# At two joins, token tiles finished one after the other, transposed between the last two weights' products, with three engines in written order

## Chip, cores and metric

The kernel runs on one core of one Trainium2 chip. The metric is the device time of one execution in microseconds (us); the median of several runs is compared. Engine names in the profile: PE is TensorE's products, PEld its weight loads, DVE is VectorE, ACT is ScalarE, POOL is GpSimd, SP is the queue that issues most transfers.

## Reference

Two layers over 512 tokens of 1024 values, all in float32. Each sub-layer is `x <- LayerNorm(ALPHA * x + sublayer(x))`. Layer 0 is a gated DeltaNet mixer and a dense SwiGLU; layer 1 is an S5 state-space mixer and a top-2-of-8 mixture of SwiGLU experts.

```python
def layer_norm(x, g, b):
    mu = mean(x); var = mean((x - mu)**2)
    return (x - mu) * rsqrt(var + LN_EPS) * g + b

def swiglu(x, w1, w3, w2):
    return (silu(x @ w1) * (x @ w3)) @ w2

# layer 0
h = gdn_mixer(x, ...)                        # ends in: o @ w_out
x = layer_norm(ALPHA * x + h, g00, b00)      # first join
f = swiglu(x, w1, w3, w2)                    # ends in: hidden @ w2
x = layer_norm(ALPHA * x + f, g01, b01)      # second join
# layer 1
h = s5_mixer(x, ...)                         # begins with: x @ s5_w_in
...
```

## The kernel before

Tokens lie in four tiles of 128 rows (`L.r[t]`, 128 x 1024 each). Every float32 operand of a product is kept as two parts: a high part (`hi`, fp32r, written by ScalarE, L68 or L73 for weights) and a low part (`lo` = value - high, written by VectorE, L69 or L76). A product of two such operands is three TensorE products (`mm3`, L128 to L130): high x high, high x low, low x high.

Weights come in 1 MB blocks of 128 x 2048. SP loads one into a `wraw` buffer (L104, three buffers here), then `wsplit` writes `whi` and `wlo` from it (two places each, so a block's high part can only be written when the products with the block two before it are done). `wload` does all of it.

At both places that the text calls joins, a matrix product ends a sub-layer and another begins the next. At the first join the last two blocks of `w_out` (high and low parts of the attention output `oT`, in the buffers `aTh` and `aTl`) give the right half of each row, at L166 and L167; then `ffn_first` (L803) starts the feed-forward layer with its first two weight blocks, f = 0 and 1. At the second join the last two blocks of `w2` end the feed-forward layer (`ffn_last`, L854) and `s5` (L1059) starts with two blocks of `s5_w_in`.

The function `two` (L181) is the join:

- it multiplies tiles 0 and 1 with both weights, then calls `res` (residual add and statistics, L692 and L727) and `ln_rows` (L752: some ten steps on one column, L734 to L750, then the row itself, L754) for them;
- it multiplies tiles 2 and 3, and turns tiles 0 and 1 with `ln_cols` (L771): 16 transposes of 128 x 128 (L781) into four PSUM buffers, and per 128 columns a ScalarE step that applies gain and offset (L785, into one of four `tmp`), the high part (L68) and the low part (L69) into `aTh` and `aTl`. These two have one place each; at the first join it is the place of `oT`'s parts;
- it calls `res` and `ln_rows` for tiles 2 and 3, which `ln_cols` turns later, when the next products are half through (the second half of `ffn_first` and of `s5`). A half is 96 products of 256 columns.

The scheduler, a list scheduler that fills each engine's instruction stream by priority and its own cost model, sets the order on all engines. Into the same streams it puts two other things near the first join. One is `ln_own` (L788): the row tiles times gain plus offset, L790 and L791, which the next residual needs and nothing before it. The other is `s5_prep` (L878), woven with the feed-forward layer by `weave`: powers of complex numbers on VectorE (L916 to L926), a chain of 113 GpSimd steps from the cosine on (L957 to L968, and L981 to L983), then on VectorE products `u` (L1021, L1023) and `w1` (L1025). The large tile `w1` of L1010 has the name of the GpSimd chain's scratch `w1` (L955), and one place with it: its first write waits for the chain's last read of the scratch (L965).

Each engine works off its stream in order; an instruction waits for the semaphores of what it needs, and all behind it wait with it.

Of the kernel before, what the change touches and what calls it, by code (L numbers as in the profile page):

```python
# [10 lines left out]
F32 = mybir.dt.float32  # L11
FR = mybir.dt.float32r
# [3 lines left out]
AF = mybir.ActivationFunctionType  # L16
# [3 lines left out]
P = 128  # L20
# [6 lines left out]
PE, DVE, ACT = (getattr(mybir.EngineType, n) for n in ("PE", "DVE", "Activation"))  # L27
# [31 lines left out]
class Builder:  # L59
# [82 lines left out]
    def build(self):  # L142
        tc, i = self.tc, self.i
        sb = lambda name, **k: tc.tile_pool(name=name, bufs=1, reuse_waits="tile", **k)
        with ExitStack() as es:
            self.wp = es.enter_context(sb("wp"))
            self.wpools = [(self.wp, dict(raw=2, hi=2, lo=2), None)]
            self.wcount = dict(raw=0, hi=0, lo=0)
            self.early = []
            self.share, self.after = 0, None  # L150
            self.cp = es.enter_context(sb("const"))
            self.pp = es.enter_context(tc.tile_pool(name="psum", bufs=1, space=bass.MemoryType.PSUM))
            act = es.enter_context(ExitStack())
            self.ap_ = act.enter_context(sb("act", side="right"))
            with sb("gdn") as self.gp:
                oT, ps0 = self.gdn()
            w = [self.wload(i["w_out"][2 + q]) for q in range(2)]
            self.rp = es.enter_context(sb("row"))
            self.wmore(es, "wmid", 1, 0, 0)
            r = self.rows("xp")  # L160
            L = self.ln_begin(r, 0)
            with sb("ffn") as self.fp, sb("prep") as self.sp:
                ps1 = [self.psum("pa") for t in range(4)]
                for t in range(4):
                    self.residual(L, t, 0, ps0[t], ALPHA)
                res = lambda t: self.residual(L, t, 1, ps1[t], ALPHA)  # L166
                self.two(lambda ts: self.tok_mm(ps1, oT, w, ts), res, L)  # L167
                first = self.ffn_first(L)
                self.weave((self.ffn(L, first), 1.0), (self.s5_prep(), PREP))
                L = self.ffn_last()  # L170
            with sb("s5") as self.sp:
                glu = self.s5(L)
            with sb("moe") as self.mp, ExitStack() as ws:
                self.wmore(ws, "wx", *WX)
                self.glu(L, *glu)
                act.close()
                self.share = SHARE
                with sb("mx", side="right") as self.mx:
                    self.moe(self.L3)

    def two(self, mm, res, L):  # L181


        mm((0, 1))
        for t in (0, 1):
            res(t)
            self.ln_rows(L, t)
        mm((2, 3))
        self.ln_cols(L, 0)
        for t in (2, 3):  # L190
            res(t)
            self.ln_rows(L, t)

    def consts(self):
        nc, cp = self.nc, self.cp
# [573 lines left out]
            g.tensor_add(r, r, L.gr[:, 1])  # L769

    def ln_cols(self, L, half, tag="acc"):  # L771
        s, v, pe = self.nc.scalar, self.nc.vector, self.nc.tensor
        if half == 0:
            L.xT = tuple(self.ap_.tile([P, KB, T], FR, name=n, tag=n, bufs=1) for n in ("aTh", "aTl"))
        cs = slice(256 * half, 256 * half + 256)
        for b in range(4):
            ps = self.psum(tag, (P, 2, 256))
            for j in range(2):
                k = 2 * b + j
                for t in range(2):  # L780
                    pe.transpose(ps[:, j, t * P:(t + 1) * P], L.r[2 * half + t][:, k * P:(k + 1) * P], self.ident)  # L781
            for j in range(2):
                k = 2 * b + j
                tmp = self.rp.tile([P, 256], F32, name="tmp", bufs=4)
                s.activation(tmp, ps[:, j], AF.Identity, scale=L.gc[:, 0, k:k + 1], bias=L.gc[:, 1, k:k + 1])  # L785
                self.split(tmp, L.xT[0][:, k, cs], L.xT[1][:, k, cs])

    def ln_own(self, L, t):  # L788
        v = self.nc.vector
        v.tensor_mul(L.r[t], L.r[t], L.gr[:, 0])  # L790
        v.tensor_add(L.r[t], L.r[t], L.gr[:, 1])  # L791
# [8 lines left out]
                         k == 0, k == KB - 1)  # L800
                yield 650 * (cs.stop - cs.start) // 512

    def ffn_first(self, L):  # L803

        w = [self.wload(self.i["ffn13"][f]) for f in range(2)]
        ps = [[self.psum("pa") for _ in range(2)] for f in range(2)]
        for half in range(2):
            if half:
                self.ln_cols(L, 1)
            for f in range(2):  # L810
                for _ in self.ffn_up(w[f], L.xT, ps[f], slice(256 * half, 256 * half + 256)):
                    pass
        return ps
# [43 lines left out]
    def ffn_last(self):  # L857

        py = [self.psum("acc") for _ in range(4)]
        for _ in self.ffn_down(py, self.ffn_w2(1, 1, 0), 0, range(4)):  # L860
            pass
        w = [self.ffn_w2(1, 1, f0) for f0 in (4, 8)]

        def mm(tiles):
            for n in range(2):
                for _ in self.ffn_down(py, w[n], 4 + 4 * n, tiles):
                    pass
        self.two(mm, lambda t: self.residual(self.L2, t, 1, py[t], 1.0), self.L2)
        return self.L2

# [183 lines left out]
                                          ap=[[128, 8], [3584, 16], [1, 128]]), tp[:, e].rearrange("p c t -> p (c t)"))  # L1056
            yield 2000

    def s5(self, L):  # L1059


        S = SimpleNamespace(un=self.sp.tile([P, 16, 8, 16], F32, name="un"), c={}, U={}, X={}, y={})
        ps = [[self.psum("pa", (P, 2, 256)) for _ in range(2)] for _ in range(2)]
        w = [self.wload(self.i["s5_w_in"][Q]) for Q in range(2)]
        S.c[0] = self.s5_load(0)
        for half in range(2):
            if half:
# [390 lines left out]
    def moe(self, L):  # L1458
# [28 lines left out]
        with self.order(DVE, ACT):  # L1487
# [24 lines left out]
            rows(0)  # L1512

            ov, two, rem, rc, a, b, bq, t0 = (c8(x) for x in ("ov", "two", "rem", "rc", "a", "b", "bq", "t0"))
            v.tensor_scalar(two, q, float(PAIRS), None, op0=OP.is_lt)
            v.scalar_tensor_tensor(ov, two, -float(RM), n, op0=OP.mult, op1=OP.add)
            v.tensor_scalar(rem, ov, 128.0, None, op0=OP.is_gt)
            for m in (256.0, 384.0):
# [460 lines left out]
```

## Time and profile before

| | us |
|---|---|
| runs (median, lowest, highest of 3) | 1459.57, 1453.78, 1462.43 |
| the profiled execution, its own time | 1465.39 |
| its span, first to last instruction | 1463.4 |
| TensorE busy (PE) | 1411.5 (96%) |
| VectorE busy | 964.5 (66%) |
| ScalarE busy | 701.5 (48%) |
| GpSimd busy | 547.0 (37%) |
| mean granted TensorE clock | 0.976 |

Times of the profile count from the span's first instruction. The first join lies at about 345 to 396 us, the feed-forward layer reaches to about 740, the second join lies at about 740 to 792. A busy time is the union of an engine's instructions in the stretch. The granted clock is 1.00 at 2.4 GHz and 0.50 at 1.2 GHz. In a timeline, what stands in brackets is the time for which the engine was idle before the row, and the instruction that ended the idle time.

### The profile page before, as it was taken

The page shows a single profiled execution, that of the slowest core. Times are in us where ns is not written, and L with a number is a line of the kernel's source. Part 1 is how long each engine was busy: PE and PEld are TensorE (multiplying, and loading weights), DVE is VectorE, ACT ScalarE, POOL GpSimd, SP SyncE. Part 2 cuts the span into 40 slices and gives each one's busy share as a digit, 9 for nine tenths or more (in the row PEclk, how much of TensorE's full clock was granted, in tenths as well). Part 3 has the DMA queues.
Part 4 walks back from the last instruction along what each step waited for, and adds up shares of the span by engine and source line. Part 5 has one row for each costly group of instructions (what it writes and reads, how often), then busy time and mean ns, then how long its engine had stood idle before and what let it go on. Part 6 is the DMA issues. An engine that isn't in the chain of part 4 may idle for free. (4 is left out here: it accounts for less than half of the span.)

```text
span 1463.4 us, 26997 instructions
## 1 busy us (share of the span) xinstructions
PE 1411.5 (96%) x10724; PEld 1178.7 (81%) x10724; DVE 964.5 (66%) x1675; ACT 701.5 (48%) x938; POOL 547.0 (37%) x660
## 2 busy tenths in 40 slices
PE   8999999999999999999999999998999999999994
PEld 5878787777877777777878878788998899999883
DVE  5757587637976666653356486686864587778793
ACT  5636365433534434443234323255764577776540
POOL 1000000000787773000000830036975579988250
PEclk9989999879999999999999999999999999999997
DMA  5221222205334454443235766378975799997861
GB/s 205 62 66 62 66 64 66 68 30 182 116 117 152 155 165 153 144 134 123 90 132 222 220 218 240 123 297 329 393 277 202 265 393 398 363 383 280 279 224 38
DMA packets 97747, 274.15 MB, mean 187 GB/s; under 512 B 33472, under 2 KB 51024, under 8 KB 78032
## 3 DMA queue, kind: packets, MB, share of 16 engines
q1 hardware_dynamic: 92688, 256.29, 48.9%
q0 software_dynamic: 4928, 16.08, 3.8%
q8 instruction: 86, 1.41, 0.4%
q14 instruction: 45, 0.37, 0.1%
HBM read 241.47 MB, written 30.88 MB: 186 GB/s over the span
## 5 line engine op out<-in xcount | busy, mean ns | idle before, releaser
L76 DVE TENSOR_TENSOR wlo<-wraw,whi 128x2048 fp32r<-128x2048 f32 (+2 forms) x165 | 353.2, 2147 | 150.2 <-ACT whi L73 150.2
L73 ACT ACTIVATE whi<-wraw 128x2048 fp32r<-128x2048 f32 (+1 forms) x165 | 309.1, 1877 | 219.3 <-PE acc L130 88.6
L128 PE MATMUL pa<-whi,xgh 128*128 128x256 f32 x704 | 205.3, 292 | 0.3 <-ACT whi L73 0.3
L129 PE MATMUL pa<-wlo,xgh 128*128 128x256 f32 x704 | 197.9, 281 | 4.9 <-POOL wlo L78 4.9
L130 PE MATMUL pa<-whi,xgl 128*128 128x256 f32 x704 | 198.2, 282 | 0.9 <-DVE xgl L69 0.9
L78 POOL TENSOR_TENSOR wlo<-wraw,whi 128x384 fp32r<-128x384 f32 x73 | 172.4, 2381 | 44.5 <-ACT whi L73 41.6
L128 PE MATMUL pa<-aTh,whi 128*128 128x512 f32 (+1 forms) x400 | 154.4, 389 | 1.6 <-ACT aTh L68 1.5
L130 PE MATMUL pa<-aTh,wlo 128*128 128x512 f32 (+1 forms) x400 | 154.2, 387 | 1.3 <-DVE wlo L76 1.3
L129 PE MATMUL pa<-aTl,whi 128*128 128x512 f32 (+1 forms) x400 | 153.2, 385 | 1.5 <-DVE aTl L69 1.5
L128 PEld LDWEIGHTS pa<-whi,xgh 128*128 128x128 f32 x704 | 133.1, 189 | 11.2 <-issue 8.1
L128 PE MATMUL acc<-whi,hh 128*128 128x512 f32 x352 | 140.9, 401 | 0.0
L130 PE MATMUL acc<-whi,hl 128*128 128x512 f32 x352 | 139.0, 397 | 0.8 <-DVE hl L69 0.7
L129 PEld LDWEIGHTS pa<-wlo,xgh 128*128 128x128 f32 x704 | 133.5, 190 | 7.0 <-POOL wlo L78 5.2
L129 PE MATMUL acc<-wlo,hh 128*128 128x512 f32 x352 | 138.9, 395 | 0.0
L130 PEld LDWEIGHTS pa<-whi,xgl 128*128 128x128 f32 x704 | 133.1, 189 | 1.3 <-DVE xgl L69 1.3
L128 PE MATMUL acc<-aTh,whi 128*128 128x512 f32 x240 | 101.2, 422 | 7.3 <-ACT whi L68 6.9
L129 PE MATMUL acc<-aTl,whi 128*128 128x512 f32 x240 | 101.0, 421 | 0.0
L130 PE MATMUL acc<-aTh,wlo 128*128 128x512 f32 x240 | 100.1, 417 | 0.0
L129 PEld LDWEIGHTS pa<-aTl,whi 128*128 128x128 f32 x400 | 76.5, 192 | 17.5 <-DVE aTl L69 2.0
L128 PEld LDWEIGHTS pa<-aTh,whi 128*128 128x128 f32 x400 | 76.1, 191 | 17.8 <-ACT aTh L68 2.1
L130 PEld LDWEIGHTS pa<-aTh,wlo 128*128 128x128 f32 x400 | 76.4, 192 | 16.9 <-DVE wlo L76 2.2
L130 PEld LDWEIGHTS acc<-whi,hl 128*128 128x128 f32 x352 | 65.7, 188 | 18.0 <-DVE hl L69 2.9
(513 smaller groups left out, 2860.1 us busy)
## 6 DMA issues: line engine op xcount, KB each, us to landing
wraw<-in_m SPq DMA_DIRECT2D x95, 1024.0 KB
wraw<-in_ffn SPq DMA_DIRECT2D x30, 1024.0 KB
r<-in_m SPq DMA_DIRECT2D x22, 1024.0 KB
wraw<-in_w_in SPq DMA_DIRECT2D x15, 1024.0 KB
grow<-in_m SPq DMA_DIRECT2D x11, 1024.0 KB
c<-s_d SPq DMA_DIRECT2D x8, 1024.0 KB
wraw<-in_w_glu SPq DMA_DIRECT2D x8, 1024.0 KB
c<-s_d SPq DMA_DIRECT2D x8, 768.0 KB
```

The costliest lines, as they stand in the source:

```text
L73: self.nc.scalar.activation(hi, src, AF.Copy)
L76: self.lo = self.nc.vector.tensor_sub(lo[:, :m], src[:, :m], hi[:, :m].bitcast(F32))
L78: self.nc.gpsimd.tensor_sub(lo[:, m:], src[:, m:], hi[:, m:].bitcast(F32))
L128: mm(out, a[0], b[0], start=start, stop=False)
L129: mm(out, a[0], b[1], start=False, stop=False)
L130: return mm(out, a[1], b[0], start=False, stop=stop)
```

## The change

`two` now takes the products per weight (`mm(tiles, n)`), loads the next two weights itself, and writes three engines' instructions in a fixed relative order (`self.order(DVE, PE, ACT)`). Tile 0 is multiplied with both weights, then normed; then tile 1. Tiles 2 and 3 are multiplied with the first weight; the 16 transposes of tiles 0 and 1 come next, all of them before the columns; then the next weight's split and three of four column steps, the products with the second weight, the second next weight's high part, the fourth column step, both residuals, its low part, and the row norms. Instructions from outside the block (`ln_own`, `s5_prep`) are still put between these by the scheduler.

```diff
-    def two(self, mm, res, L):
-        mm((0, 1))
-        for t in (0, 1):
-            res(t)
-            self.ln_rows(L, t)
-        mm((2, 3))
-        self.ln_cols(L, 0)
-        for t in (2, 3):
-            res(t)
-            self.ln_rows(L, t)
+    def two(self, mm, res, L, nxt, tag):
+        v, s = self.nc.vector, self.nc.scalar
+        raws = [self.wraw(x) for x in nxt]
+        w = [(self.wtile("hi", FR), self.wtile("lo", FR)) for _ in nxt]
+        mms = lambda *a: [None for _ in mm(*a)]
+        hi = lambda n: s.activation(w[n][0], raws[n], AF.Copy)
+        lo = lambda n: v.tensor_sub(w[n][1], raws[n], w[n][0].bitcast(F32))
+        with self.order(DVE, PE, ACT):
+            for t in (0, 1):
+                mms((t,), 0)
+                mms((t,), 1)
+                res(t)
+                self.ln_rows(L, t)
+            mms((2, 3), 0)
+            hi(0)
+            lo(0)
+            cols = self.ln_turned(L, 0, tag)
+            for b in range(3):
+                next(cols)
+            mms((2, 3), 1)
+            hi(1)
+            next(cols)
+            for t in (2, 3):
+                res(t)
+            lo(1)
+            for t in (2, 3):
+                self.ln_rows(L, t)
+        return w
...
     def ln_cols(self, L, half, tag="acc"):
+        for _ in self.ln_turned(L, half, tag):
+            pass
+
+    def ln_turned(self, L, half, tag):
         s, v, pe = self.nc.scalar, self.nc.vector, self.nc.tensor
...
-        for b in range(4):
-            ps = self.psum(tag, (P, 2, 256))
+        pt = [self.psum(tag, (P, 2, 256)) for b in range(4)]
+        for b, ps in enumerate(pt):
             for j in range(2):
...
+        for b, ps in enumerate(pt):
             for j in range(2):
                 k = 2 * b + j
                 tmp = self.rp.tile([P, 256], F32, name="tmp", bufs=4)
                 s.activation(tmp, ps[:, j], AF.Identity, scale=L.gc[:, 0, k:k + 1], bias=L.gc[:, 1, k:k + 1])
                 self.split(tmp, L.xT[0][:, k, cs], L.xT[1][:, k, cs])
+            yield
```

`ffn_first` and `s5` get the two split weights from `two` instead of loading them. In SP's queue this moves the row constants of the second norm behind three blocks of the feed-forward layer, and the fourth block of `s5_w_in` ahead of six loads of S5 tables; all else there stays.

Three places show the move in the built program. Line numbers in rows of the changed kernel are its own (L190 is L76 of before, L816 and L817 are L790 and L791, L938 to L948 are L916 to L926, L956 is L934, L1043, L1045, L1047 are L1021, L1023, L1025).

**PE, first join.** `pa_3508` and `pa_3509` are the right halves of tiles 0 and 1; `whi_3474`, `wlo_3475` the first, `whi_3480`, `wlo_3481` the second weight. In the kernel before, PE's stream reads here:

```order
L128 MATMUL pa_3508<-whi_3474,aTh_3240 128x512
L129 MATMUL pa_3508<-wlo_3475,aTh_3240 128x512
L130 MATMUL pa_3508<-whi_3474,aTl_3241 128x512
L128 MATMUL pa_3509<-whi_3474,aTh_3240 128x512
L129 MATMUL pa_3509<-wlo_3475,aTh_3240 128x512
L130 MATMUL pa_3509<-whi_3474,aTl_3241 128x512
L128 MATMUL pa_3508<-whi_3480,aTh_3240 128x512
L129 MATMUL pa_3508<-wlo_3481,aTh_3240 128x512
L130 MATMUL pa_3508<-whi_3480,aTl_3241 128x512
```
In the changed kernel it reads:

```order
L129 MATMUL pa_3508<-wlo_3475,aTh_3240 128x512
L130 MATMUL pa_3508<-whi_3474,aTl_3241 128x512
L128 MATMUL pa_3508<-whi_3474,aTh_3240 128x512
L129 MATMUL pa_3508<-wlo_3475,aTh_3240 128x512
L130 MATMUL pa_3508<-whi_3474,aTl_3241 128x512
L128 MATMUL pa_3508<-whi_3480,aTh_3240 128x512
L129 MATMUL pa_3508<-wlo_3481,aTh_3240 128x512
L130 MATMUL pa_3508<-whi_3480,aTl_3241 128x512
L128 MATMUL pa_3508<-whi_3480,aTh_3240 128x512
```
The second weight is met after tile 0's own products with the first, instead of after those of both tiles: 7 products behind the first that starts at 345.19 us in the profile of before, where it was 19.

**DVE, first join, behind the norm of tile 1.** `wlo_3525` (before: `wlo_3725`) is the low part of the next weight, the rows with `aTl` are the low splits of the turned columns, `pw`, `t1`, `t2` belong to the S5 preparation, the rows with `grow` are the own scaling. In the kernel before, VectorE's stream reads here:

```order
L908 TENSOR_TENSOR cn_4036<-cn_4036,rr_4016 128x32
L76 TENSOR_TENSOR wlo_3725<-wraw_3722,whi_3724 128x2048
L692 SCALAR_TENSOR_TENSOR r_3491<-r_3491,pa_3510 128x512
L692 SCALAR_TENSOR_TENSOR r_3491<-r_3491,pa_3511 128x512
L727 BN_STATS b6_3501<-r_3491 128x6 x2
L734 BN_AGGR lnst_3500<-b6_3501 128x2
L76 TENSOR_TENSOR wlo_3731<-wraw_3728,whi_3730 128x2048
L69 TENSOR_TENSOR aTl_3643<-tmp_3649,aTh_3642 128x256
L69 TENSOR_TENSOR aTl_3643<-tmp_3653,aTh_3642 128x256
L69 TENSOR_TENSOR aTl_3643<-tmp_3662,aTh_3642 128x256
L69 TENSOR_TENSOR aTl_3643<-tmp_3666,aTh_3642 128x256
```
In the changed kernel it reads around the first low part:

```order
L816 TENSOR_TENSOR r_3490<-r_3490,grow_3498 128x1024
L190 TENSOR_TENSOR wlo_3525<-wraw_3520,whi_3524 128x2048
L938 TENSOR_TENSOR pw_4045<-er_4017,cn_4039 128x32
L939 TENSOR_TENSOR pw_4045<-er_4017,sn_4038 128x32
L817 TENSOR_TENSOR r_3490<-r_3490,grow_3498 128x1024
L943 TENSOR_TENSOR t1_4050<-pw_4045 128x32
L944 TENSOR_TENSOR t2_4051<-pw_4045 128x32
L956 TENSOR_SCALAR rr_4019<-pw_4045 128x32
L816 TENSOR_TENSOR r_3490<-r_3490,grow_3498 128x1024
L69 TENSOR_TENSOR aTl_3631<-tmp_3652,aTh_3630 128x256
L945 TENSOR_TENSOR pw_4045<-t1_4050,t2_4051 128x32
L817 TENSOR_TENSOR r_3490<-r_3490,grow_3498 128x1024
```
Both next low parts stood ahead of the splits, four of which came in a row; the own scaling came after all eight. Now all four steps of the own scaling of tiles 0 and 1 stand ahead of the second split, and 33 small steps of the preparation stand between the first low part and the eighth split.

**DVE, first join, second half.** The splits of tiles 2 and 3 in the changed kernel, with `u1`, `u2` and `w1` of the preparation:

```order
L1043 TENSOR_TENSOR u1_4626<-pw_4045,bb_4625 128x4x128
L1045 TENSOR_TENSOR u2_4627<-pw_4045,bb_4625 128x4x128
L69 TENSOR_TENSOR aTl_3631<-tmp_3857,aTh_3630 128x256
L69 TENSOR_TENSOR aTl_3631<-tmp_3861,aTh_3630 128x256
L1047 TENSOR_TENSOR w1_4638<-u1_4626,u2_4627 128x4x128
L816 TENSOR_TENSOR r_3491<-r_3491,grow_3498 128x1024
L69 TENSOR_TENSOR aTl_3631<-tmp_3865,aTh_3630 128x256
L69 TENSOR_TENSOR aTl_3631<-tmp_3869,aTh_3630 128x256
L69 TENSOR_TENSOR aTl_3631<-tmp_3873,aTh_3630 128x256
L69 TENSOR_TENSOR aTl_3631<-tmp_3877,aTh_3630 128x256
```
In the kernel before, the same splits, from the third on:

```order
L69 TENSOR_TENSOR aTl_3643<-tmp_3852,aTh_3642 128x256
L69 TENSOR_TENSOR aTl_3643<-tmp_3856,aTh_3642 128x256
L926 TENSOR_TENSOR pw_4042<-t1_4047,t2_4048 128x32
L791 TENSOR_TENSOR r_3491<-r_3491,grow_3498 128x1024
L69 TENSOR_TENSOR aTl_3643<-tmp_3865,aTh_3642 128x256
L69 TENSOR_TENSOR aTl_3643<-tmp_3869,aTh_3642 128x256
L921 TENSOR_TENSOR t1_4047<-pw_4042 128x32
L69 TENSOR_TENSOR aTl_3643<-tmp_3878,aTh_3642 128x256
L69 TENSOR_TENSOR aTl_3643<-tmp_3882,aTh_3642 128x256
L922 TENSOR_TENSOR t2_4048<-pw_4042 128x32
```
The `w1` step stands between the second and the third split now. Before, it came after the eighth split and two further low parts.

## Rows read from the trace of the kernel before

**Rows 1.** The page, part 1: engine, busy us (share of the span), instructions.
```profile
PE 1411.5 (96%) x10724; PEld 1178.7 (81%) x10724; DVE 964.5 (66%) x1675; ACT 701.5 (48%) x938; POOL 547.0 (37%) x660
```

**Rows 2.** Busy time by stretch: length, then PE, PEld, DVE, ACT, POOL; clock, DMA.
```profile
366.51:382.76 16.25, 14.02 (x114) 13.43 (x113) 16.21 (x57) 8.12 (x18) 7.47 (x15) 1.00 0.36 129
382.76:396.40 13.64, 12.79 (x102) 12.10 (x101) 13.40 (x34) 11.11 (x21) 13.06 (x29) 1.00 0.10 30
420.00:440.00 20.00, 18.72 (x82) 14.49 (x80) 17.33 (x24) 8.18 (x8) 16.13 (x32) 1.00 0.59 182
440.00:740.00 300.00, 300.00 (x1421) 239.50 (x1420) 163.24 (x229) 110.77 (x153) 100.86 (x253) 1.00 0.43 138
760.18:776.50 16.32, 14.14 (x102) 13.27 (x101) 15.64 (x40) 9.63 (x21) 0.00 (x0) 0.90 0.94 379
777.83:791.60 13.77, 12.96 (x106) 12.21 (x105) 7.41 (x12) 9.70 (x25) 0.00 (x0) 1.00 0.37 138
```

**Rows 3.** Timelines of PE, ACT, DVE at the second weight: start, us, engine, line.
```profile
345.19 0.40 PE L130 MATMUL pa<-whi,aTl 128*128 128x512 f32 x1
...
349.64 0.39 PE L128 MATMUL pa<-whi,aTh 128*128 128x512 f32 x1
...
345.39 1.92 ACT L73 ACTIVATE whi<-wraw 128x2048 fp32r<-128x2048 f32 x1 [4.74 <-PE acc L130]
...
347.34 2.29 DVE L76 TENSOR_TENSOR wlo<-wraw,whi 128x2048 fp32r<-128x2048 f32 x1 [2.05 <-ACT whi L73]
```

**Rows 4.** Timeline of DVE, the first join: small steps, splits, own scaling.
```profile
361.16 0.19 DVE L889 TENSOR_TENSOR ar<-scst,dt 128x32 f32<-128x32 f32 x1
361.26 0.18 DVE L890 TENSOR_TENSOR ai<-scst,dt 128x32 f32<-128x32 f32 x1
361.48 0.18 DVE L893 TENSOR_SCALAR k<-ai 128x32 f32<-128x32 f32 x1
...
370.91 1.42 DVE L69 TENSOR_TENSOR aTl<-tmp,aTh 128x256 fp32r<-128x256 f32 x4
...
378.55 1.21 DVE L790 TENSOR_TENSOR r<-r,grow 128x1024 f32<-128x1024 f32 x1
```

**Rows 5.** Timeline of DVE, the first join: residuals, statistics, rows.
```profile
366.01 1.38 DVE L692 SCALAR_TENSOR_TENSOR r<-r,pa 128x512 f32<-128x512 f32 x2 [0.60 <-PE pa L130]
367.31 1.28 DVE L727 BATCH_NORM_STATS2 b<-r 128x6 f32<-128x512 f32 x2
...
377.58 0.80 DVE L754 TENSOR_SCALAR r<-r,lnst 128x1024 f32<-128x1024 f32 x1
```

**Rows 6.** Timelines of ACT, POOL, DVE; last, DVE groups of 374.95 to 416.07.
```profile
363.19 1.28 ACT L906 ACT_TABLE_LOAD   x1
...
374.95 0.40 POOL L957 TENSOR_TENSOR w<-cn 128x32 f32<-128x32 f32 x1 [9.44 <-ACT cn L910]
...
395.44 2.25 POOL L981 TENSOR_TENSOR g<-rot,zz 128x4 f32<-128x4 f32 x1
...
409.80 0.24 POOL L981 TENSOR_TENSOR g<-rot,zz 128x32 f32<-128x32 f32 x1
...
416.07 0.25 POOL L965 TENSOR_TENSOR w<-w,w 128x32 f32<-128x32 f32 x1
...
395.32 2.30 DVE L76 TENSOR_TENSOR wlo<-wraw,whi 128x2048 fp32r<-128x2048 f32 x1
...
416.35 0.79 DVE L1025 TENSOR_TENSOR w<-u,u 128x512 f32<-128x512 f32 x1 [6.84 <-POOL w L965]
...
L790 DVE TENSOR_TENSOR r<-r,grow 128x1024 f32<-128x1024 f32 x4 | 4.9, 1224 | 0.0
```

**Rows 7.** Timeline of DVE, the second join: the second weight's low part.
```profile
742.30 1.76 DVE L76 TENSOR_TENSOR wlo<-wraw,whi 128x1536 fp32r<-128x1536 f32 x1 [7.66 <-ACT whi L73]
```

**Rows 8.** Busy time by stretch, the second join, at its half-rate stretch.
```profile
761.91:765.32 3.41, 1.23 (x8) 0.78 (x6) 3.41 (x5) 3.41 (x9) 0.00 (x0) 1.00 0.99 393
765.33:768.74 3.41, 3.41 (x16) 3.28 (x16) 3.41 (x12) 3.15 (x8) 0.00 (x0) 0.50 1.01 425
```

More of the change, by code (lines that the diff above doesn't have):

```diff
@@ L166, in build @@
                 res = lambda t: self.residual(L, t, 1, ps1[t], ALPHA)
-                self.two(lambda ts: self.tok_mm(ps1, oT, w, ts), res, L)
-                first = self.ffn_first(L)
+                mm = lambda ts, n: self.chain(self.tok_mms(ps1, oT, w, ts, range(4 * n, 4 * n + 4)))
+                first = self.ffn_first(L, self.two(mm, res, L, [i["ffn13"][f] for f in range(2)], "acc"))
                 self.weave((self.ffn(L, first), 1.0), (self.s5_prep(), PREP))
-                L = self.ffn_last()
+                L, w = self.ffn_last()
             with sb("s5") as self.sp:
-                glu = self.s5(L)
+                glu = self.s5(L, w)
             with sb("moe") as self.mp, ExitStack() as ws:
@@ L801, in ffn_up, with ffn_first @@
                 yield 650 * (cs.stop - cs.start) // 512
-    def ffn_first(self, L):
-        w = [self.wload(self.i["ffn13"][f]) for f in range(2)]
+    def ffn_first(self, L, w):
         ps = [[self.psum("pa") for _ in range(2)] for f in range(2)]
@@ L862, in ffn_last @@
         w = [self.ffn_w2(1, 1, f0) for f0 in (4, 8)]
[L864 to L869, printed above, removed]
+        return self.L2, self.two(lambda ts, n: self.ffn_down(py, w[n], 4 + 4 * n, ts),
+                                 lambda t: self.residual(self.L2, t, 1, py[t], 1.0), self.L2,
+                                 [self.i["s5_w_in"][Q] for Q in range(2)], "pa")
     def s5_prep(self):
@@ L1057, in s5_prep, with s5 @@
             yield 2000
-    def s5(self, L):
+    def s5(self, L, w):
         S = SimpleNamespace(un=self.sp.tile([P, 16, 8, 16], F32, name="un"), c={}, U={}, X={}, y={})
         ps = [[self.psum("pa", (P, 2, 256)) for _ in range(2)] for _ in range(2)]
-        w = [self.wload(self.i["s5_w_in"][Q]) for Q in range(2)]
         S.c[0] = self.s5_load(0)
```

## The prediction

> **What bounds the kernel now.** I read the page first, then the busy time by stretch, then the timelines of the engines at the two joins. TensorE is busy for 96% of the span [rows 1], so what counts is where it is not. From 440 to 740 us, the feed-forward stage between the joins, it is busy for all 300.00 of 300.00 us [rows 2]: a delay made at the first join cannot be made up before the second. At the first join it idles 16.25 - 14.02 = 2.2 us in the first half and 13.64 - 12.79 = 0.85 us in the second, and 1.3 us between 420 and 440; at the second join 2.2 and 0.8 us, and it runs one stretch of 3.4 us at half rate there. VectorE is the engine to watch: in the two halves of the first join it is busy for 16.21 of 16.25 and 13.40 of 13.64 us [rows 2]. Anything put in front of a step that TensorE needs delays TensorE there.
>
> All times below are on the clock of the profiled execution. Its own time is 1465.39 us, 5.8 above the median of the three runs (1459.57); I work out a difference and add it to the median.
>
> **First join: the products.** Products of 512 columns start 0.234 us apart (345.19 to 349.64, 19 products [rows 3]). Before, 19 products of the first weight stand between 345.19 and the first of the second weight, and the second weight's low part is ready at 347.34 + 2.29 = 349.63 [rows 3]: just in time. Now tile 0 takes both weights in turn, and only 7 products are left of its first. TensorE comes to the second weight at 346.8; the high part is there at 345.39 + 1.92 = 347.3, the low part at 349.63. New wait: 0.5 + 2.1 = **2.6 us**. Nothing hides it, since the high part itself waits for a buffer that the earlier products hold [rows 3]. The 67 products up to the new place of the transposes then end at 345.19 + 67 x 0.234 + 2.6 = 363.5, the transposes (1.8 us, as before, only moved) at 365.3, the last 24 products at 370.9.
>
> **First join: what was to be hidden beneath these 24 products isn't.** The split values of the turned tokens go into the buffers aTh and aTl, which have one place, and the 24 products still read from it. ScalarE's first store there must wait for 370.9, and all behind it on ScalarE too. VectorE meanwhile works off its new queue, which the order above shows. From 365.3 to the last of the eight low splits it holds: 4 steps of the rows' own scaling, 1.21 each [rows 4], of which the last 0.07 lie beside the next step (as at 366.01 + 1.38 and 367.31 [rows 5]) = 4.6; the low part of the next weight, 2.2; 8 splits at 0.34 = 2.8 (four take 1.42 [rows 4]); 33 small steps of the S5 preparation, which start 0.1 to 0.21 apart [rows 4], at 0.17 = 5.6. Together 15.2, so the last split ends near 380.5. Then two residuals with their statistics, 2.4 [rows 5], three small steps, and the second weight's low part, 2.2: **385.6**. TensorE, back at 370.9, finishes f = 0 behind the splits and needs this low part for f = 1: it has 44 of 96 products left, 0.12 us apart, and ends the half at 390.9. At full pace it would be 382.4, so it idles 8.5 us where it idled 2.2.
>
> Then come the row norms of tiles 2 and 3: 46 small steps, interleaved with preparation, at 0.13, and 2 x 0.74 for the rows [rows 5]: 7.4, until 393.0. TensorE waits 1.7 us for them before the last transposes, and starts the second half at 395.0.
>
> **First join: a wait that was hidden now isn't.** In the second half VectorE has the step that writes the large w1 of the preparation in front of six of the eight splits. w1 has the place of a scratch that GpSimd uses; before, VectorE waited 6.84 us there until 416.35 [rows 6], with all splits long done and little behind it. Now it comes to it near 393.0 + 2.8 (two small steps, copies, two products of 0.6, two splits) = 395.8. When does GpSimd let go? It started at 374.95, when the cosine left ScalarE, and its last read began at 416.07: 41.1 us for 113 steps. Undisturbed it does 30 in 6.3 us (409.80 to 416.07), so 113 take 24.4. The other 16.7 us went beneath VectorE's steps with two operands in SBUF: one of its steps took 2.25 us beside a low part of 2.30 [rows 6]. There were about 20.5 us of these (8 of the own scaling 9.8 [rows 6], 2 low parts 4.6, ten splits 4.7, 2 products 1.4), so about 0.8 us was lost for each. After the change the cosine comes once the first weight's high part (363.7 to 365.6), one turn step (0.5), a table load (1.3 [rows 6]) and the sine are through, near 367.5. Then 24.4 + 0.8 x 12.5 (3 own scalings 3.7, the low parts 1.1 and 2.3, ten splits 4.0, the products 1.4) = 34.4: 402.0. VectorE stands for **6.2 us**. The six splits come behind it and a further own scaling, so TensorE, which has done some 25 products and stopped near 398.0, goes on at 404.4 and ends at 404.4 + 71 x 0.12 = 412.9. Before it was 396.40. **First join: +16.5.** The bounds of this wait: nothing, if GpSimd runs undisturbed (367.5 + 24.4 = 391.9, before 395.8), and 12.8, if it takes 41.1 again. I take 6.2, as the share of disturbed time is measured for these very steps.
>
> The Trainium skill ("SBUF — State Buffer", Who interferes with whom) speaks against this change harder: a VectorE instruction with two SBUF inputs and a GpSimd instruction that reads SBUF share a port that one holds for its whole length. By that rule the share would be 1.0, the wait 8.6 and the whole 2.4 us more. The rows of this trace show 0.8 over the stretch, and I keep that.
>
> **Between the joins.** The 1.3 us at 420 to 440 should go, since VectorE has done that preparation by then: -1.3. Otherwise full pace: 15.2 us arrive at the second join. In SP's queue the row constants for the second norm now go behind three weight loads; they are used 300 us later, at no cost. The fourth S5 weight goes ahead of six loads of S5 tables; at most 1 MB ahead of data first used 12 us later: nothing.
>
> **Second join.** aTh is free there, so the splits do run beneath the products. Second weight: its low part is ready at 742.30 + 1.76 = 744.1 [rows 7], TensorE comes to it after 12 instead of 48 products, some 2.8 us after the previous weight's last: 0.5 wait. VectorE's queue after the transposes: own scaling 1.14, low part 2.2, four splits, one scaling, two splits, two scalings, two splits: 9.8 us from the first of them. TensorE is back after 4.2 us (18 products) and meets the splits late: I count 2.8 us of waits, then 1.9 us for the second low part, which stands behind both residuals; the second half 1.6 with its transposes. Sum 6.8. Before it was 2.2 + 0.8, and the stretch 765.33 to 768.74 at half rate, where 16 products took the place of 31 [rows 8]: 15 x 0.11 = 1.6. So 4.6 before, and **+2.2**.
>
> **The clock.** The half-rate stretch stood right behind 1.23 us of work in 3.41 [rows 8]. Now TensorE stands for 6 us in one place and for 2 to 3 in others. Where it waits for VectorE afterwards too, half rate costs nothing. I take one further stretch that hurts: +1.6; bounds 0, since stalls of 2.2 us at the first join before were followed by no half rate there, and 6.6 for four.
>
> **Sum:** 16.5 - 1.3 + 2.2 + 1.6 = **+19.0 us**, so 1478.6 us. Range of this case alone: 19 - 6.2 - 1.6 to 19 + 6.6, cut to 1471 to 1485.
>
> **Rivals.**
> - *The queue costs, GpSimd doesn't.* GpSimd is through when VectorE comes to w1. For: undisturbed it is done at 391.9. Against: VectorE's two-operand steps are as dense as before. Then 19.0 - 6.2 - 1.6 = 11.2: 1470.8 us. Chance 0.17.
> - *Faster.* The idle time at the joins goes: 2.2 + 0.85 + 2.2 + 0.8 and the 1.6 of half rate = 7.7: 1451.9 us. It decides whether VectorE gets the low part and eight splits (5.0 us) done while TensorE has its last products (5.6 us at the first join, 4.2 at the second). Alone in the queue they would fit; with four own scalings and 33 small steps among them they don't, and at the first join the store waits anyway. Chance 0.05.
> - *The waits only change places.* The moved work costs about what it saves, or the small steps run at 0.1 in a row and the splits come near enough in time: within 7 us, taken as 1462. Chance 0.09.
> - *The clock as well.* Four stretches at half rate and GpSimd as slow as before: 19.0 + 6.6 + 5.0 = 30.6: 1490.2 us. Chance 0.07.
>
> **Numbers.** The forecast has a chance of 0.62. What a measurement can tell from no change is about 0.5%, 7.3 us. Slower by more: the forecast, the first rival (most of it) and the last: 0.85. Within: 0.10. Faster: 0.05. The range 1465 to 1486 takes in the forecast with its bounds and the first rival and leaves out the faster rival, the slowest, and half of the third.
>
> **What would show it.** Right: TensorE waiting about 2 us for a low part near 347; VectorE waiting for GpSimd at the w1 step before six splits, near 396 to 402, and TensorE behind it; the wait for the next weights' low parts (2.7 and 1.9 us) late in each first half; 440 to 740 as busy as before, 15 us later. Wrong: no wait of VectorE for GpSimd inside the join, the first store of split values before the last product, or second halves that end less than 10 us later than before.

## The result, and the profile after

The changed kernel takes 1477.14 us in the median of four runs (1472.41 to 1486.27), the kernel before 1460.62 in four. The ratio of their runs is 1.0131 (95% interval 1.0088 to 1.0174): 19 us slower, between 13 and 25; the two medians are 16.5 apart. The profiled execution spans 1479.7 us, 16.3 more than before.

Spans of single executions scatter by some 10 us, since TensorE has stretches at half rate in the first mixer, ahead of the joins (from 230 to 320 us its mean granted clock is 0.85 in the kernel before, 0.91 in the changed one and 1.00 in seven others): the joins begin between 329 and 346 us in the thirteen profiles of this study. So I compare stretches that start and end with the same product of TensorE, counted from zero in the order of their starts: 2596 is among the last products of the left halves, 2815 and 2918 lie within 2 us of the ends of the two halves of the first join, 3200 is in the feed-forward stage, 4440 to 4900 hold the second join, 4900 to 5600 the start of the S5 stage. The stretches (us) are of one profiled execution each. The time is the median of the runs; the ratio is that of the runs to those of the kernel before on the same chip, whose medians lie between 1456.78 and 1460.62. Single runs differ by 10 us and more, so the ratio need not be that of the two medians (for `join2` these give 1.0072). The profiled execution of `late` is its slowest run, 1478.80 us, and begins the join latest, at 345.7; its clock at the join itself is 1.00.

| kernel | 2596 to 2815 | to 2918 | to 3200 | together | 4440 to 4900 | to 5600 | time | ratio (95%) |
|---|---|---|---|---|---|---|---|---|
| before | 41.4 | 14.0 | 62.5 | 118.0 | 80.4 | 50.0 | 1460.62 | 1 |
| changed | 54.6 | 20.3 | 60.7 | 135.6 | 81.4 | 50.1 | 1477.14 | 1.0131 (1.0088 to 1.0174) |
| scratch | 51.7 | 13.5 | 60.7 | 125.9 | 80.1 | 55.4 | 1471.33 | 1.0087 (1.0056 to 1.0117) |
| held | 50.4 | 12.6 | 74.7 | 137.7 | 81.3 | 50.1 | 1478.12 | 1.0127 (1.0091 to 1.0164) |
| pair | 50.9 | 23.5 | 60.7 | 135.2 | 80.9 | 53.7 | 1473.43 | 1.0098 (1.0063 to 1.0132) |
| lo1 | 51.5 | 23.3 | 60.7 | 135.6 | 79.9 | 55.2 | 1478.21 | 1.0134 (1.0094 to 1.0174) |
| held_scratch | 50.4 | 12.6 | 62.6 | 125.6 | 79.9 | 57.9 | 1467.69 | 1.0059 (1.0032 to 1.0087) |
| all | 46.7 | 12.9 | 62.5 | 122.1 | 78.7 | 58.0 | 1463.44 | 1.0043 (1.0007 to 1.0078) |
| early | 46.3 | 12.9 | 62.5 | 121.6 | 83.6 | 54.8 | 1467.20 | 1.0069 (1.0037 to 1.0102) |
| late | 41.6 | 14.3 | 62.6 | 118.5 | 80.2 | 57.6 | 1463.67 | 1.0038 (1.0004 to 1.0071) |
| bheld | 41.5 | 12.6 | 61.8 | 115.9 | 80.4 | 50.5 | 1457.72 | 0.9986 (0.9952 to 1.0020) |
| mix | 42.6 | 12.6 | 61.6 | 116.8 | 80.2 | 54.2 | 1458.07 | 0.9999 (0.9970 to 1.0028) |
| join2 | 41.4 | 14.0 | 62.5 | 118.0 | 81.4 | 52.6 | 1467.28 | 1.0033 (1.0002 to 1.0063) |

The first two rows say where the time went: 13.2 + 6.3 = 19.5 us at the first join, 1.8 back right behind it, 1.0 at the second.

How far single stretches can be trusted is seen from kernels that have the same instructions in the same order there. From product 4900 on, the streams of TensorE, VectorE, ScalarE and GpSimd are the same in eight kernels (before, changed, `scratch`, `held`, `pair`, `held_scratch`, `bheld`, `join2`), and that stretch takes 50.0 to 57.9 us in them. The busy time of it in the changed kernel and in `held_scratch`:

```profile
818.01:868.07 50.06, 46.76 (x703) 41.40 (x702) 29.63 (x43) 18.73 (x32) 41.53 (x56) 1.00 0.74 245
```

```profile
798.41:856.34 57.93, 52.90 (x704) 46.31 (x702) 32.94 (x49) 18.84 (x32) 43.51 (x57) 0.86 0.69 221
```

(Length, PE, PEld, DVE, ACT, POOL, clock, DMA.) So no difference of a few us in the last column is put down to an edit. At the second join the changed kernel, `scratch`, `held`, `held_scratch` and `join2` are the same in this sense and take 79.9 to 81.4 us, against 80.4 before: the 1.0 us there is within that scatter.

The busy time by stretch of the changed kernel (length, PE, PEld, DVE, ACT, POOL, clock, DMA), first the two halves of the first join, then the stretches that answer to [rows 2]:

```profile
370.94:393.92 22.98, 16.68 (x97) 14.85 (x97) 22.35 (x97) 7.86 (x15) 21.90 (x78) 0.85 0.20 75
393.92:415.31 21.39, 15.74 (x115) 15.30 (x114) 14.86 (x22) 11.10 (x21) 17.57 (x48) 0.84 0.07 20
420.00:440.00 20.00, 20.00 (x87) 16.12 (x86) 11.92 (x20) 7.09 (x7) 16.05 (x38) 1.00 0.62 198
440.00:755.00 315.00, 315.00 (x1486) 251.59 (x1485) 169.55 (x234) 114.60 (x158) 98.34 (x232) 1.00 0.43 136
```

TensorE is idle for 22.98 - 16.68 = 6.3 us in the first half and 5.65 in the second, and its granted clock is 0.85 and 0.84 there, where before it was 1.00. VectorE is full in the first half (22.35 of 22.98) and not in the second (14.86 of 21.39): there it waits itself. From 420 to the second join TensorE doesn't stop, so nothing more of the loss comes back there.

The timeline of TensorE at its waits in the first join (start, us, engine, line, and in brackets the idle time and what ended it), against [rows 3]:

```profile
345.34 0.50 PE L128 MATMUL pa<-whi,aTh 128*128 128x512 f32 x1 [0.36 <-ACT whi L73]
347.67 0.80 PE L129 MATMUL pa<-wlo,aTh 128*128 128x512 f32 x1 [1.83 <-DVE wlo L76]
...
370.94 0.50 PE L128 MATMUL pa<-aTh,whi 128*128 128x256 f32 x2 [0.34 <-ACT aTh L68]
...
385.87 0.58 PE L130 MATMUL pa<-aTh,wlo 128*128 128x256 f32 x1 [2.42 <-DVE wlo L190]
...
393.92 1.91 PE L805 MATMUL acc<-ident,r 128*128 128x128 f32 x16
...
404.65 0.58 PE L129 MATMUL pa<-aTl,whi 128*128 128x256 f32 x1 [5.22 <-DVE aTl L69]
```

In turn: the second weight met too early, the low part behind splits and residuals, the splits behind the w1 step. The timeline of VectorE shows what held these:

```profile
383.54 2.27 DVE L190 TENSOR_TENSOR wlo<-wraw,whi 128x2048 fp32r<-128x2048 f32 x1
...
392.09 0.81 DVE L773 TENSOR_SCALAR r<-r,lnst 128x1024 f32<-128x1024 f32 x1
...
396.24 0.85 DVE L69 TENSOR_TENSOR aTl<-tmp,aTh 128x256 fp32r<-128x256 f32 x2 [0.94 <-ACT aTh L68]
402.27 0.79 DVE L1047 TENSOR_TENSOR w<-u,u 128x512 f32<-128x512 f32 x1 [5.19 <-POOL w L987]
402.99 1.22 DVE L816 TENSOR_TENSOR r<-r,grow 128x1024 f32<-128x1024 f32 x1
404.13 1.94 DVE L69 TENSOR_TENSOR aTl<-tmp,aTh 128x256 fp32r<-128x256 f32 x4
```

And that of GpSimd, the first step of its chain and the last read of the scratch, which answer to [rows 6]:

```profile
367.32 1.12 POOL L980 TENSOR_TENSOR w<-sn 128x32 f32<-128x32 f32 x1 [40.37 <-ACT sn L928]
...
401.99 0.25 POOL L987 TENSOR_TENSOR w<-w,w 128x32 f32<-128x32 f32 x1
```

Behind each of the three long waits TensorE works at half rate. The busy time of these stretches:

```profile
347.67:351.14 3.47, 3.47 (x9) 2.76 (x9) 2.93 (x5) 0.00 (x0) 0.00 (x0) 0.52 0.92 297
385.87:392.00 6.13, 6.13 (x29) 6.13 (x30) 6.13 (x46) 0.00 (x0) 6.05 (x28) 0.50 0.49 171
404.65:409.07 4.42, 4.42 (x21) 4.42 (x22) 4.42 (x8) 2.91 (x5) 3.87 (x8) 0.51 0.02 2
```

The granted clock is 0.50 to 0.52, the 1.2 GHz level. Length times one minus clock is what each lost, an estimate: 1.7, 3.1 and 2.2 us.

### The profile page after: what moved, and what is told of

It reads as the page before. It is cut to its first block, busy times and chain, and to the rows that moved or that the text cites. A ratio compares the mean times of both kernels' runs of the same rounds, so it can differ in the third digit from the quotient of the medians.

```text
span 1479.7 us, 26994 instructions
## 1 busy us (share of the span) xinstructions
PE 1415.9 (96%) x10724; PEld 1181.8 (80%) x10724; DVE 970.0 (66%) x1675; ACT 703.1 (48%) x938; POOL 547.0 (37%) x660
## 5 line engine op out<-in xcount | busy, mean ns | idle before, releaser
L76 DVE TENSOR_TENSOR wlo<-wraw,whi 128x2048 fp32r<-128x2048 f32 (+3 forms) x161 | 343.3, 2139 | 153.4 <-ACT whi L73 153.2
L73 ACT ACTIVATE whi<-wraw 128x2048 fp32r<-128x2048 f32 (+2 forms) x161 | 301.4, 1876 | 205.1 <-PE acc L130 71.7
```

The source lines that it names most:

```text
L73: self.nc.scalar.activation(hi, src, AF.Copy)
L76: self.lo = self.nc.vector.tensor_sub(lo[:, :m], src[:, :m], hi[:, :m].bitcast(F32))
```

## Experiments

**scratch.** Does the wait for GpSimd hold the second half? Its scratch gets names of its own; VectorE's, TensorE's and ScalarE's streams stay as they are.

```diff
-        z0, z1, w0, w1 = cn, sn, sm("w0"), sm("w1")
+        z0, z1, w0, w1 = cn, sn, sm("w0s"), sm("w1s")
```

> The changed kernel with GpSimd's two scratch tiles named w0s and w1s, so that VectorE's large w1 no longer shares a place with one of them; the streams of the other engines stay as they are. Theory A (VectorE's order at the first join, and the wait for GpSimd in it): the 5.2 us wait of VectorE in front of the w1 step goes, TensorE's idle 5.2 us in the second half of the first join with it, and the half-rate stretch behind it (20 products at 0.213 instead of 0.118 us, 2.1 us): 7 us less, 1470 us, the second half ending near 408 instead of 415.3. Rival B (another step of the preparation waits for GpSimd's chain as well, so that the wait only moves): 0 to 1 us less, 1477. Rival C (clock alone: TensorE stays at half rate there for other reasons): 5 us less, 1472.

Theory A. The timeline of VectorE shows the w1 step without a wait, and that of GpSimd its chain still running 7 us later:

```profile
383.62 0.82 DVE L69 TENSOR_TENSOR aTl<-tmp,aTh 128x256 fp32r<-128x256 f32 x2
384.36 0.74 DVE L1047 TENSOR_TENSOR w<-u,u 128x512 f32<-128x512 f32 x1
```

```profile
391.78 0.25 POOL L987 TENSOR_TENSOR w0s<-w0s,w1s 128x32 f32<-128x32 f32 x1
```

The second half takes 13.5 us instead of 20.3 (6.8 less, 7 expected). Nothing else in there waited for GpSimd: a shared name alone made this wait. The first half is 2.9 shorter too, half of that because the half-rate stretch at the second weight does not occur in this execution. The ratio falls from 1.0131 to 1.0087, 6.4 us, but the two intervals overlap; up to product 3200 it is 9.7 us less, and the stretches from 4440 on give 4.0 of that back, where the streams are the same in both kernels.

**held.** What do the steps from outside the block cost in VectorE's queue? `split` keeps its last instruction, and the own scaling and the preparation's first VectorE steps are queued behind it.

```diff
...
             if half:
                 self.ln_cols(L, 1)
+                self.hold = self.last
...
+        with self.behind(self.hold):
             v.tensor_mul(L.r[t], L.r[t], L.gr[:, 0])
...
+        with self.behind(self.hold):
             v.tensor_mul(ar, lre, dt)
             v.tensor_mul(ai, lim, dt)
```

> The changed kernel with the own scaling and the start of the S5 preparation put behind the last low split of the first join, so that VectorE's stream there holds the block's own steps alone. Theory A (foreign steps in VectorE's queue, and the wait for GpSimd): first half, the second weight's low part is ready at 384.2 instead of 385.8 (six columns by 375.4 as ScalarE stores them, its next high part 1.9, two columns, 379.3, residuals 2.7, low part 2.2), row norms end near 390 instead of 392.9; second half without the wait, 14.6 us: it ends at 404 to 407 instead of 415.3. After the join the moved steps cost 0 to 3. Sum 8 to 11 us less, 1467. Rival B (the buffer of the turned columns with its one place sets the pace, ScalarE's stores come too late whatever VectorE does): the first half stays within 1 us, the second half gains what the wait for GpSimd was worth, 5 to 7 us less, 1471.

At the join theory A holds: 63.0 us to product 2918 instead of 74.9, 11.9 less. But nothing is gained, which neither theory had (theory A had 0 to 3 us behind the join): the next stage takes 14 us more. The timelines of VectorE and TensorE in the feed-forward stage say why:

```profile
438.58 0.79 DVE L1050 TENSOR_TENSOR w<-u,u 128x512 f32<-128x512 f32 x1 [9.78 <-POOL w L990]
```

```profile
439.52 0.30 PE L1065 MATMUL pa<-ident,w 128*128 128x128 f32 x1 [4.81 <-DVE w L1050]
441.54 0.90 PE L1065 MATMUL pa<-ident,w 128*128 128x128 f32 x3 [1.72 <-DVE w L1050]
```

The wait for GpSimd has moved along with the preparation, and there TensorE's own transposes of w1 and the next weights' splits stand behind it.

**pair.** Does the wait at the second weight cost what the profile shows?

```diff
+            mms((0, 1), 0)
             for t in (0, 1):
-                mms((t,), 0)
                 mms((t,), 1)
```

> The changed kernel with the first weight's products of tiles 0 and 1 both ahead of the second weight's (at both joins), all else as it is. Theory A: the wait for the second weight (0.36 and 1.83 us) goes at the first join and the nine products at half rate behind it (1.6 us): everything behind comes 3.7 us earlier, 1473.5 us. Rival B (the norm of tile 1 is late then, since both tiles end their products close together): it ends at about 359.6, with the transposes at 359.4; 2 to 3.5 us less, 1474 to 1475. Rival C (VectorE's queue decides anyway, and it starts no earlier): no gain, 1477.

The wait goes, and the first half takes 3.7 us less; 3.2 of it come back in the second (23.5 instead of 20.3): 135.2 against 135.6 up to product 3200, rival C by the stretches. In ScalarE's stream two columns and a table load now stand ahead of the sine, so that GpSimd's chain begins 31.0 us behind product 2596 where it was 28.1, and VectorE waits longer for it:

```profile
392.48 0.79 DVE L1047 TENSOR_TENSOR w<-u,u 128x512 f32<-128x512 f32 x1 [7.08 <-POOL w L987]
```

The median, 1473.43, is that of theory A, but the interval of the ratio (1.0098) overlaps that of the changed kernel, so that the times can't decide here.

**lo1.** The second next low part moves ahead of the residuals.

```diff
+            lo(1)
             for t in (2, 3):
                 res(t)
-            lo(1)
```

> The changed kernel with the second next weight's low part ahead of the residuals of tiles 2 and 3 instead of behind them. Theory A (VectorE's queue as a whole is what is late; the row norms of tiles 2 and 3 come behind both and end at the same 393): TensorE no longer waits 2.4 us for the low part, but waits for the row norms before the next transposes: the first half of the first join ends within 1 us of 393.9; with fewer products at half rate in it, but no gain; 1477, 0 to 1.5 us less over both joins. Rival B (the wait costs what the profile shows, 2.4 us and the 29 products at half rate behind it, 2.7 us): 3 to 5 us less, 1473.

No gain, as theory A said, but not by its mechanism. The first half does end 3.1 us earlier, and the second takes 3.0 more. It isn't the row norms that are next in line, it is GpSimd again, 6.6 us now:

```profile
392.32 0.79 DVE L1047 TENSOR_TENSOR w<-u,u 128x512 f32<-128x512 f32 x1 [6.61 <-POOL w L987]
```

So GpSimd's chain sets the end of the second half: in `pair` and in `lo1`, what is gained ahead of it only lengthens VectorE's wait.

**held_scratch.** Both edits together.

> The changed kernel with both edits at once: own scaling and preparation behind the join, and GpSimd's scratch under names of its own. Theory A (the wait of VectorE for GpSimd's chain goes wherever the w1 step goes, with what stands behind it; the foreign steps cost the first half 2.7 us by themselves): the join as in the kernel with the steps held back alone (from product 2596 to 2918 of the program 63.0 us, against 74.9 in the changed kernel), and the 14 us lost in the feed-forward stage gone (product 2918 to 3200 in 61 to 63 us instead of 74.7): 11 to 12 us less than the changed kernel, 1465. Rival B (the preparation costs that much in the feed-forward stage whatever it waits for, since VectorE is full there): product 2918 to 3200 stays above 70, 1475 or more.

Theory A: 63.0 us at the join and 62.6 behind it. 125.6 against 135.6 is 10 us less (11 to 12 expected); the ratio falls by 0.0072, 10.5 us, and the intervals just do not overlap. The held steps cost the feed-forward stage 1.9 us; the rest of the 14 had been the wait.

**all, early, late.** What is left is 7.6 us at the join: 9.0 in the first half, less 1.4 in the second. All three kernels have the four edits so far; `early` splits the second next weight ahead of the columns; `late` does so at the first join alone (its tag is `acc`), and puts the transposes, which `ln_turned` issues ahead of the columns, behind the last 24 products there. Of `late`:

```diff
...
             mms((2, 3), 0)
+            if tag == "acc":
+                mms((2, 3), 1)
             hi(0)
             lo(0)
+            if tag == "acc":
+                hi(1)
+                lo(1)
             cols = self.ln_turned(L, 0, tag)
...
```

> The same with the first weight's products of tiles 0 and 1 ahead of the second weight's, and the second next low part ahead of the residuals. Theory A (with GpSimd's chain out of the way, the gains of these two edits stay, 3.7 and 2.7 us): product 2596 to 3200 in 118 us, as in the kernel before (118.0); 1460 us, no difference from before to be measured. Rival B (ScalarE's stores into the one place of the turned columns bound the first half, and the next weight's high part behind six of them): they keep 2 to 3 us of it, product 2596 to 2815 above 46; 1463.

> The same again, with the second next weight split before all columns on ScalarE and VectorE, instead of between the third and the fourth pair of them. Theory A (what is then left of the change is only the order of TensorE's own work): product 2596 to 2815 in 42 us (41.4 before, 44 in the kernel before this edit), the second half 12.6, product 2918 to 3200 in 61.5; 116 us against 118.0 before, 1458. Rival B (the high part waits for the last product in any case and then delays all eight columns by its 1.9 us): no gain or 2 us more than without this edit, 46.

> The kernel with all four edits (steps held back, scratch renamed, first weight's products of tiles 0 and 1 first, low part ahead of the residuals), and at the first join the 16 transposes put back behind the last 24 products, with both next weights split ahead of the columns. Theory A (at the first join the transposes are TensorE's only work that can lie beneath the second next high part and the first stores, since these wait for the 24 products; put ahead of the products they save nothing and leave 1.9 us bare): product 2596 to 2815 in 42 to 43 us (46.7 with all four edits, 41.4 before); 2918 a little later for the row norms, 13 to 14; product 2596 to 3200 in 118 to 119, 3 to 4 less than with the four edits; 1460. Rival B (the columns stored one by one set the pace, wherever the transposes are): 46 as before this edit, no gain, 1463.5.

`all` and `early` went as rival B said (46.7 and 46.3 in the first half; at the second join `early` takes 83.6, `all` 78.7), `late` as theory A said at the join (41.6; 41.4 before). The timelines of TensorE behind the last 24 products, of `early` and of `late` (L812 are the transposes):

```profile
361.06 0.50 PE L128 MATMUL pa<-aTh,whi 128*128 128x256 f32 x2 [2.90 <-ACT aTh L68]
362.82 0.58 PE L129 MATMUL pa<-aTl,whi 128*128 128x256 f32 x1 [1.26 <-DVE aTl L69]
```

```profile
370.96 1.91 PE L812 MATMUL acc<-ident,r 128*128 128x128 f32 x16
374.02 0.50 PE L128 MATMUL pa<-aTh,whi 128*128 128x256 f32 x2 [1.16 <-ACT aTh L68]
```

And the busy time of the stretch from there to the end of the half, in the same order:

```profile
358.15:376.70 18.55, 14.39 (x97) 14.18 (x96) 13.05 (x35) 8.88 (x17) 0.00 (x0) 0.82 0.19 70
```

```profile
370.96:387.40 16.44, 14.02 (x113) 13.52 (x112) 11.47 (x30) 8.89 (x17) 0.00 (x0) 1.00 0.35 125
```

The next high part and the first store wait for the 24 products, since their places are still read. While ScalarE does them, the transposes are TensorE's only work. Ahead of the products they save nothing, and leave that time bare: 4.2 us idle (18.55 - 14.39) with a clock of 0.82, against 2.4 and 1.00. From product 2596 to 2815 the difference is 4.6 us (46.3 and 41.6).

A second place for the turned columns, by their shape 32 KB more per partition, was not tried, so what it would give stays open.

In time `late` gains nothing on `all` (1463.67, 1463.44), although its join is 3.6 us shorter and its second join only 1.5 longer. I leave that open; it is within the intervals, and the expected 1460 is neither shown nor excluded.

**bheld.** The kernel before with its own scaling and preparation held and the scratch renamed.

> The kernel before, with the same two edits: own scaling and preparation held behind the last low split of the first join, and GpSimd's scratch under names of its own. Theory A (VectorE's queue at the join costs the kernel before 2.2 and 0.85 us, and 1.3 at 420 to 440): product 2596 to 3200 in 114.5 to 116 us (118.0 before); 2 to 3.5 us less, 1456, which is less than a measurement can tell. Rival B (the moved steps meet VectorE in the feed-forward stage): up to 3 us more there, no gain.

115.9 us at the join, 2.1 less, as theory A said; in time 0.9986 (0.9952 to 1.0020), no difference.

**mix and join2.** `mix` is `bheld` with the order of `all` at the second join; `join2` is the change at the second join alone.

> The first join as in the kernel before, with the own scaling and the preparation held behind it and the scratch renamed; the second join in the changed order with the first weight's products of tiles 0 and 1 first and the low part ahead of the residuals. Theory A (the two joins differ in the buffer: at the second it is free, and there the order pays once the waits at both next weights are gone): product 2596 to 3200 in 115.9 us and product 4440 to 4900 in 78.7 (118.0 and 80.4 before): 3.8 us less than before, 1455. Rival B (what is gained at the second join is lost behind it, as the S5 stage waits for its tables): 1 to 2 us less, 1457.

> The change at the second join alone; the first join as in the kernel before. Theory A (the loss lies at the first join): product 2596 to 3200 in 118 us as before, product 4440 to 4900 in 81.4 (80.4 before): 1 us more than before, 1459.5, not to be told from no change. Rival B (the measured difference includes more at the second join or behind it than this profile shows): 3 us more or above, 1462.

The times decide neither. `join2` takes what theory A said at both joins, 118.0 and 81.4 us, and 2.6 more than before behind the second, where its streams are those of the kernel before and of the changed one, which takes 50.1; by its ratio it loses 4.8 us (0.3 to 9.2), which holds theory A's 1 us and rival B's 3. `mix` gains 0.2 instead of 1.7 at the second join and takes 4.2 more behind it, and is even with the kernel before (the interval, 0.9970 to 1.0028, just holds theory A's 3.8 us less too). No version here beats the kernel before by more than a measurement can tell.

Whether the order costs anything behind the second join is not shown: 52.6 and 54.2 us lie inside the 50.0 to 57.9 that the same streams take. One difference of order that is there in `lo1`, `all`, `early`, `late` and `mix` is in the timelines of VectorE and GpSimd, where the scheduler has put the next low part behind the first scan of the S5 stage. First those of `mix`, then GpSimd's same step in the changed kernel:

```profile
787.79 2.76 DVE L76 TENSOR_TENSOR wlo<-wraw,whi 128x2048 fp32r<-128x2048 f32 x1
```

```profile
788.37 3.33 POOL L1306 TENSOR_TENSOR ta<-X,c 128x512 f32<-128x512 f32 x1
```

```profile
819.45 1.27 POOL L1291 TENSOR_TENSOR ta<-X,c 128x512 f32<-128x512 f32 x1
```

GpSimd's step takes 3.33 us beside the low part and 1.27 without it. TensorE waits for the steps behind it, and the first 100 products from 4900 on take 8.2 us in `mix`, 7.2 in the changed kernel; but 9.0 in `scratch`, which has the old order and this step at 1.29 us. So what the low part's new place costs stays open.

## Why the prediction was right, point by point

Forecast 1478.6, measured 1477.14; forecast +19.0, by the ratio +19, by the medians +16.5. Part of the agreement is luck. Of the single times: this execution reached the join 2.0 us earlier than the one of before (product 2596 at 339.2 instead of 341.2), and the first half-rate stretch took 1.7 of it back.

- **The products.** 2.6 us of wait forecast, 0.36 + 1.83 = 2.2 measured. The half-rate stretch behind it was not forecast at this place.
- **What was to be hidden isn't.** The first store starts at 370.47, as the 24 products end. TensorE is back at 370.94 (forecast 370.9), the second low part is ready at 383.54 + 2.27 = 385.8 (385.6), the row norms end at 392.9 (393.0). The half was to end at 390.9 and TensorE to wait for the norms; it ends at 393.9 without that wait, since 29 products at half rate took its place, 3.1 us for 1.7.
- **The wait that was hidden.** VectorE comes to the w1 step at 397.1 (forecast 395.8), GpSimd lets go at 402.24 (402.0), so that it stands 5.2 us instead of 6.2; TensorE goes on at 404.65 (404.4). GpSimd took 34.9 us, by the share of 0.8 it was to be 34.4. By the steps counted in the forecast the share is (34.9 - 24.4) / 12.5 = 0.84. From the rule of the Trainium skill ("SBUF — State Buffer", Who interferes with whom) that one side holds the shared port for the whole of an instruction, I had estimated a share of 1.0 and 2.4 us more; over the whole chain the trace shows less. `scratch` shows the size: 6.8 us with the half rate behind the wait.
- **Between the joins.** -1.3 forecast, 62.5 to 60.7 measured, and 440 to 755 as busy as before.
- **Second join.** +2.2 forecast, +1.0 measured, and with the same streams -0.5 to +1.0 in other executions, so the term is not confirmed. The waits for the splits and the next high part are there, but smaller (1.8 us together, 2.8 forecast), and a wait of 1.9 us for the second low part is not in this trace. A half-rate stretch, which the forecast had only before, is there again: the granted clock is 0.71 from 785 to 790 us. TensorE's waits in the first half are these:

```profile
780.34 0.39 PE L130 MATMUL pa<-whi,aTl 128*128 128x256 f32 x1 [0.37 <-DVE aTl L69]
...
781.68 0.39 PE L128 MATMUL pa<-whi,aTh 128*128 128x256 f32 x1 [0.61 <-ACT whi L189]
782.58 0.39 PE L128 MATMUL pa<-whi,aTh 128*128 128x256 f32 x1 [0.51 <-ACT aTh L68]
...
783.40 0.39 PE L130 MATMUL pa<-whi,aTl 128*128 128x256 f32 x1 [0.32 <-DVE aTl L69]
```

- **The clock.** The term that was sized wrongly: "one further stretch that hurts: +1.6". There were three, 7.0 us, of which the last (2.2) and the first (1.7) counted in full and the second with 1.4, 5.3 in all. Terms that came out smaller (the two waits by 0.4 and 1.0, the second join by 1.2, the stage between by 0.5) made up for most of it. So the sum is nearer than its terms: the clock cost 3.7 us more than its 1.6, and the others about as much less.

Of the rivals, that the waits would only change places is what happened to three edits of the experiments, not to the change itself.

## What to carry to other kernels

When a join is reordered by hand, list everything that the scheduler may still put between the written steps, and where that waits: an in-order queue makes any foreign wait that of the critical path, and a scratch name shared with another engine's chain is enough for it. Ask of each piece of work that moves earlier what it was covering where it stood; transposes beneath a store that waits for a buffer cost nothing, ahead of it they cost their cover. Where several waits stand in a row against one slow chain, taking away the first shows nothing until the chain itself is out of the way. And before a few us in a later stage are put down to an edit, look at kernels with the same streams there: here they differ by 7.9 us.

## What was not expected of the hardware

After waits of 1.8, 2.4 and 5.2 us TensorE worked at a granted clock of 0.50 to 0.52 for 3.5 to 6.1 us. It is not a fixed price of a wait: of the five kernels that have the same wait at the second weight, two take 26.6 and 26.5 us from product 2596 to 2700 (the changed one and `lo1`), the other three 25.1. GpSimd's 128x512 step grew from 1.27 to 3.33 us beside one low part of VectorE, which itself took 2.76 instead of 2.29. It ends at 791.70, 1.15 us behind the low part's 790.55, about its own length alone; and the GpSimd step of 2.25 us in [rows 6] ends at 397.69, the low part beside it at 397.62. In both pairs GpSimd's step reads as if it had stood still until the low part was done, although over the whole chain the share is 0.84.
